# Trace of eight matrix products: Tile's planned order replaced by one section with hand-placed semaphores and a TensorE loop

## The chip, the core and the metric

The kernel runs on one core of one Trainium2 chip. The metric is the device time of one execution in microseconds (us). The engines are TensorE (PE, with its weight loads as PEld), VectorE (DVE), ScalarE (ACT), GpSimd (POOL) and SyncE (SP). Transfers are carried by 16 DMA engines; those that POOL issues convert float32 to bfloat16 on the way.

## The reference

```python
def reference(a, b):                       # a, b: [8, 2176, 2176] float32
    prod = np.matmul(a, b)
    traces = np.diagonal(prod, axis1=1, axis2=2).sum(axis=-1)
    return traces.astype(np.float32)       # [8]
```

The trace of a product needs no product: for each batch it is the sum over i, k of a[i, k] · b[k, i]. So every element of a and b is read once, 303 MB in all, and a has to be transposed against b.

## The kernel before, in words

A matrix of 2176 x 2176 is 17 rows of 128 partitions. For each batch the kernel loads a, transposes it on TensorE into `at` (one buffer, 17 rows of 2176), and multiplies `at` with b, summing.

**Loads.** `fetch` (L70 to L77) issues from POOL, in program order. A batch of a comes as a group of 5 rows (tile `middle`) and a group of 2 x 6 rows (tile `stage`, two buffers, used in turn by a and b); b comes the same way. A transfer of 5 rows is 2720 KB as it lands, one of 12 rows 6528 KB. The order of a batch is a5, a12, b5, b12. A tile is loaded again only when its reader is done: a's when TensorE has transposed it, b's when VectorE has multiplied it. Batch 0 begins with one row by SP (`load_first`, L88, cast on ACT and DVE). The last batch loads a as 12 rows and then 5, and b in groups of 4, 4, 4, 2, 1, 1, 1 rows (`fine`), the last row in three pieces (L273).

**Transposes.** `transpose_group` (L134) transposes 128 x 128 blocks into one of three PSUM tiles: pairs of bf16 words as float32 (L151), the odd rows of a group of b as bf16 (L175). One PSUM tile filled is one copy to `at` in `evacuate` (L117): every fourth on DVE (L121), the others on ACT (L123). A batch with groups of 5 and 6 has 26 copies, 8 for the 5 rows and 18 for the 12.

**Products.** `multiply_reduce` (L126, its work is shown as L128) multiplies and sums rows on DVE, 1.05 us per 1000 elements: the 5 rows, then the 12. It begins when all copies of the batch are done (`copies_end`). In the last batch rows 11, 12 and 13 and part of rows 15 and 16 are multiplied on TensorE instead, as 128 x 128 products summed in `trace_ps` (L287), with some unread matmuls between them (`KEEP_BUSY`). A last DVE product takes the diagonal, a matmul with ones sums over the partitions (L306), DVE adds (L309), SP stores (L312). The sums of the first seven batches pass through a matmul and a DVE addition of their own (L295, L296), which Tile places among the transposes of the last batch.

**Order.** Tile places all waits and the pools' buffers; `issue_after` fixes the order of the loads, of the DVE products after the copies and of the TensorE products. TensorE's program is written out for all eight batches.

Of the kernel before, what the change touches and what calls it, by code (L numbers as in the profile page):

```python
# [8 lines left out]


def row_groups(p, rows):

    groups, at = [], 0
    for m in rows:
        groups.append((at, m))
        at += m * p
    return groups
# [3 lines left out]
def kernel(  # L21
# [6 lines left out]
    nc = tc.nc  # L28
    P = 128
    BATCH, N, N2 = a.shape  # L30
    assert N == N2 and N % P == 0
    NT = N // P
    MOST, MID = 12, 5
# [3 lines left out]
    MUL, ADD = mybir.AluOpType.mult, mybir.AluOpType.add  # L37

    even = [5, 6, 6]
    fine = [4, 4, 4, 2, 1, 1, 1]  # L40

    a_loads = b_loads = [(1, 5), (2, 6)]
    first_loads, last_loads = [(1, 1), (1, 4), (2, 6)], [(2, 6), (1, 5)]
    for loads in (a_loads, first_loads, last_loads):
        assert sum(g * m for g, m in loads) == NT
    assert sum(even) == sum(fine) == NT

    PE_ROWS = (11, 12, 13)

    SHARED_ROW = 15  # L50
    HALF = 8 * P

    LAST_PIECES = [(6 * P, 11 * P, N), (2 * P, 2 * P, 6 * P), (0, 0, 2 * P)]

    KEEP_BUSY = {11: 7, 13: 6, SHARED_ROW: 2}

    const = ctx.enter_context(tc.tile_pool(name="const", bufs=1))
    at_pool = ctx.enter_context(tc.tile_pool(name="at_pool", bufs=1))
    stage = ctx.enter_context(tc.tile_pool(name="stage", bufs=2))
    middle = ctx.enter_context(tc.tile_pool(name="middle", bufs=1))  # L60
    single = ctx.enter_context(tc.tile_pool(name="single", bufs=1))
    psum_pool = ctx.enter_context(tc.tile_pool(name="psum", bufs=3, space=bass.MemoryType.PSUM))
    psum_small = ctx.enter_context(tc.tile_pool(name="psum_small", bufs=1, space=bass.MemoryType.PSUM))

    loaded = []

    def in_order():

        return tc.issue_after(loaded[-1].ins) if loaded else nullcontext()

    def fetch(t, src, start, g, m):

        rows = src[start:start + P * g * m, :].rearrange("(g p r) k -> p g (r k)", g=g, r=m)
        with in_order():
            issued = nc.gpsimd.dma_start(out=t.rearrange("p (g r) k -> p g (r k)", g=g), in_=rows)  # L75
        loaded.append(issued)
        return t  # L77

    def load(src, start, g, m):

        if g * m <= MID:
            t = middle.tile([P, MID, N], bf16, tag="middle")
        else:
            t = stage.tile([P, MOST, N], bf16, tag="stage")
        return fetch(t[:, 0:g * m, :], src, start, g, m)

    def load_first(src, start):

        words = stage.tile([P, MOST, N], bf16, tag="stage")
        plain = words.bitcast(f32).rearrange("p r k -> p (r k)")[:, :N]  # L90
        half = N // 2
        t = single.tile([P, 1, N], bf16, tag="single")
        nc.sync.dma_start(out=plain, in_=src[start:start + P, :])
        nc.scalar.copy(out=t[:, 0, :half], in_=plain[:, :half])  # L94
        nc.vector.tensor_copy(out=t[:, 0, half:], in_=plain[:, half:])  # L95
        return t

    per_batch = len(b_loads)
    tiles = {}

    def constants():
        identity32 = const.tile([P, P], f32, tag="identity32")
        make_identity(nc, identity32)
        identity16 = const.tile([P, P], bf16, tag="identity16")
        make_identity(nc, identity16)
        ones = const.tile([P, 1], f32, tag="ones")
        nc.vector.memset(ones, 1.0)
        sums = const.tile([P, (BATCH - 1) * per_batch], f32, tag="sums")
        late = const.tile([P, 2 * NT], f32, tag="late")
        diagonal = const.tile([P, P], bf16, tag="diagonal")  # L110
        result = const.tile([P, BATCH], f32, tag="result")
        tiles.update(ones=ones, sums=sums, late=late, result=result, diagonal=diagonal)
        tiles[f32], tiles[bf16] = identity32, identity16

    evacs = 0
    last_copy = None

    def evacuate(dst, src):
        nonlocal evacs, last_copy
        if evacs % 4 == 3:  # L120
            last_copy = nc.vector.tensor_copy(out=dst, in_=src)  # L121
        else:
            nc.scalar.copy(out=dst, in_=src)  # L123
        evacs += 1

    def multiply_reduce(x, y, acc, out=None):  # L126

        nc.vector.tensor_tensor_reduce(  # L128
            out=x if out is None else out, in0=x, in1=y, scale=1.0, scalar=0.0,
            op0=MUL, op1=ADD, accum_out=acc,  # L130
        )

    def transpose_group(at, a_t, start, m, b_groups):

        words = a_t.bitcast(f32)
        dst = at[:, :, start:start + P * m].rearrange("q v (p r) -> q v p r", r=m)
        pairs, singles = [], []
        for b_start, bm in b_groups:
            v = b_start // P
            if bm % 2 == 0:  # L140
                for t in range(bm // 2):
                    pairs.append((v + 2 * t, b_start // 2 + t, bm // 2))
            else:
                singles += [(v + r, b_start + r, bm) for r in range(bm)]

        for at0 in range(0, len(pairs), 8 // m):
            some = pairs[at0:at0 + 8 // m]
            ps = psum_pool.tile([P, 8, P], f32, tag="aT")
            for n, (v, c0, step) in enumerate(some):
                for r in range(m):  # L150
                    nc.tensor.transpose(  # L151
                        ps[:, n * m + r, :],
                        words[:, r, c0:c0 + step * (P - 1) + 1:step],
                        tiles[f32],
                    )
            if m == 1:
                v0 = some[0][0]
                evacuate(
                    dst[:, v0:v0 + 2 * len(some), :, 0].rearrange("q (n s) p -> q n s p", s=2),
                    ps.bitcast(bf16).rearrange("q n (p s) -> q n s p", s=2)[:, 0:len(some), :, :],  # L160
                )
                continue
            for n, (v, _, _) in enumerate(some):
                evacuate(
                    dst[:, v:v + 2, :, :],
                    ps[:, n * m:(n + 1) * m, :].bitcast(bf16).rearrange("q r (p s) -> q s p r", s=2),
                )
        for at0 in range(0, len(singles), 16 // m):
            some = singles[at0:at0 + 16 // m]
            ps = psum_pool.tile([P, 8, P], f32, tag="aT")  # L170
            ps16 = ps.bitcast(bf16).rearrange("q a b -> q (a b)")[:, 0:len(some) * m * P]
            ps16 = ps16.rearrange("q (n r p) -> q n r p", r=m, p=P)
            for n, (v, c0, step) in enumerate(some):
                for r in range(m):
                    last_transpose = nc.tensor.transpose(  # L175
                        ps16[:, n, r, :],
                        a_t[:, r, c0:c0 + step * (P - 1) + 1:step],
                        tiles[bf16],
                    )
            v0 = some[0][0]  # L180
            evacuate(dst[:, v0:v0 + len(some), :, :], ps16.rearrange("q n r p -> q n p r"))
        return last_transpose

    pe_work = []

    def multiply_on_pe(at, row, v, lo, hi):

        for c in range(lo, hi, P):
            pe_work.append((at[:, v, c:c + P], row[:, c:c + P]))

    def keep_pe_busy(at, v):

        x = at[:, v, :]
        pe_work.extend([(x[:, 0:P], x[:, 0:4 * P])] * KEEP_BUSY.get(v, 0))

    late = []
    ahead = None
    for bi in range(BATCH):
        last = bi == BATCH - 1
        b_groups = row_groups(P, fine if last else even)  # L200


        at = at_pool.tile([P, NT, N], bf16, tag="at")
        at_row = 0
        for g, m in last_loads if last else a_loads if bi else first_loads:
            start = at_row * P
            at_row += g * m
            if not tiles:
                a_t = load_first(a[bi], start)
                ahead = load(a[bi], start + P * m, *first_loads[1])  # L210
                with tc.issue_after(loaded[-1].ins):
                    constants()
            elif ahead is not None:
                a_t, ahead = ahead, None
            else:
                a_t = load(a[bi], start, g, m)
# [129 lines left out]
```

## Time and profile before

| what | value |
|---|---|
| median of 3 runs | 708.93 us (708.8 to 709.13) |
| span of the profiled execution, first to last instruction | 707.05 us |
| outside the span, median less span | 1.88 us |
| HBM read | 303.04 MB, 429 GB/s over the span |
| PE, PEld, DVE, ACT, POOL busy | 28%, 25%, 55%, 29%, 3% |
| mean granted TensorE clock | 0.656 |
| PE instructions, PEld instructions | 1569, 1569 |

The profile is of one execution. The time of that same execution outside its span is not recorded, so changes are counted in its span and added to the median. A row of the timeline gives start, duration, engine, line, operation, count, and in brackets the idle time before with what ended it. The chain of waits follows the end back, step by step, to what released it. The clock is the share of full speed that TensorE was granted.

### The profile page before, as it was taken

The numbers are of one execution on the slowest core, as the hardware profiler recorded it, in microseconds if no ns is written. First come the engines' busy times: TensorE is split into PE (matmuls) and PEld (weight loads), VectorE is DVE, ScalarE is ACT, GpSimd is POOL, SyncE is SP. The second block draws the span as 40 slices with busy tenths as digits, with TensorE's granted clock in tenths as the row PEclk, the third lists the DMA queues.
The fourth block names the chain that finished last, engine by engine and source line by source line (L and its number), as shares of the span: only waits on it lengthen the run. The fifth ranks groups of instructions, "written<-read, shape, count | busy, mean of one in ns | idle before, by whom it ended". The sixth has DMA issues, their size and how long they took to land.

```text
span 707.1 us, 3653 instructions
## 1 busy us (share of the span) xinstructions
PE 200.8 (28%) x1569; PEld 179.8 (25%) x1569; DVE 386.8 (55%) x98; ACT 202.9 (29%) x160; POOL 24.7 (3%) x47
## 2 busy tenths in 40 slices
PE   2235003450134501344012440134301353003806
PEld 1234002440123401243012430124301343003703
DVE  0105488154881539616397163961629627395497
ACT  2327002470024700346004350044500445002910
POOL 1000000000000000000000000000000000000100
PEclk9759555695557955678556785567755677555957
DMA  9999999999999999999999999999999999999997
GB/s 236 213 217 212 225 206 214 216 224 214 224 215 213 223 213 214 216 223 218 215 217 216 215 222 213 216 223 211 221 216 216 222 214 217 216 220 213 217 211 151
DMA packets 7698, 152.31 MB, mean 215 GB/s; under 512 B 642, under 2 KB 898, under 8 KB 1282
## 3 DMA queue, kind: packets, MB, share of 16 engines
q0 software_dynamic: 7536, 150.96, 99.6%
q1 hardware_dynamic: 146, 1.11, 0.4%
q8 instruction: 12, 0.20, 0.1%
q14 instruction: 4, 0.03, 0.0%
HBM read 303.04 MB, written 0.00 MB: 429 GB/s over the span
## 4 chain that ended last, share of the span: by engine, by line
DVE 33%; another core or an unknown queue 27%; ACT 13%; PE 12%; DMA 11%; issue 3%; POOL 0%; ACTq 0%; DVEq 0%; POOLq 0%
DVE at L128 33%; ACT at L123 13%; PE ps L151 9%; DMA t<-in_a_dram 6%; DMA shared<-in_b_dram 5%; PE ps L175 2%; DVE at L121 0%; POOL shared L75 0%; PE trace_ps L287 0%; POOL shared L273 0%; POOL identity masks.py:199 0%; POOL identity masks.py:197 0%; ACTq L123 0%; DVE diagonal L128 0%
## 5 line engine op out<-in xcount | busy, mean ns | idle before, releaser
L123 ACT COPY at<-ps 128x1536 bf16<-128x1536 bf16 (+5 forms) x158 | 200.5, 1359 | 467.2 <-DVE sums L128 308.6
L128 DVE CUSTOM_DVE_ANT_0 at<-at,t 128x10880 bf16<-128x10880 bf16 (+1 forms) x14 | 272.0, 19426 | 96.3 <-DMA t<-in_b_dram 86.6
L151 PE MATMUL ps<-identity,t 128*128 128x128 f32 x833 | 147.1, 344 | 471.6 <-DMA t<-in_a_dram 378.6
L151 PEld LDWEIGHTS ps<-identity,t 128*128 128x128 f32 x833 | 131.3, 209 | 484.6 <-issue 380.3
L121 DVE COPY at<-ps 128x1536 bf16<-128x1536 bf16 (+3 forms) x52 | 83.4, 1604 | 205.8 <-PE ps L151 152.5
L175 PE MATMUL ps<-identity,t 128*128 128x128 bf16 x646 | 45.8, 227 | 11.0 <-ACT at L123 8.6
L175 PEld LDWEIGHTS <-t 128*128 128x128 bf16 x646 | 43.1, 119 | 14.7 <-issue 14.2
L128 DVE CUSTOM_DVE_ANT_0 at<-at,shared 128x8704 bf16<-128x8704 bf16 (+4 forms) x6 | 29.9, 5001 | 1.8 <-DMA shared<-in_b_dram 1.7
L75 POOL DMA_DIRECT2D t<-in_a_dram x16 | 10.1, 637 | 294.1 <-DVE sums L128 267.4
L75 POOL DMA_DIRECT2D t<-in_b_dram x14 | 8.7, 628 | 290.8 <-PE ps L175 290.5
L287 PEld LDWEIGHTS <-at 128*128 128x128 bf16 x86 | 6.8, 112 | 24.7 <-issue 23.9
L287 PE MATMUL trace_ps<-shared,at 128*128 128x128 bf16 x71 | 5.8, 241 | 21.0 <-DMA shared<-in_b_dram 20.9
L75 POOL DMA_DIRECT2D shared<-in_b_dram x6 | 3.2, 541 | 59.3 <-DVE sums L128 38.9
L287 PE MATMUL unread<-at 128*128 128x512 bf16 x15 | 5.2, 496 | 0.0
L296 DVE TENSOR_REDUCE result<-total 1x7 f32<-1x14 f32 x1 | 0.2, 159 | 7.8 <-PE total L295 7.8
L95 DVE CAST t<-words 128x1088 bf16<-128x1088 f32 x1 | 0.7, 727 | 4.9 <-DMA words<-in_a_dram 4.9
L94 ACT CAST t<-words 128x1088 bf16<-128x1088 f32 x1 | 1.1, 1099 | 3.7 <-DMA words<-in_a_dram 3.7
L273 POOL DMA_DIRECT2D shared<-in_b_dram x3 | 1.6, 552 | 1.9 <-DMA shared<-in_b_dram 1.9
L94 ACT ACT_TABLE_LOAD x1 | 1.3, 1283 | 0.7 <-PEq L330 0.7
L128 DVE DVE_READ_ACCUMULATOR2_ANT sums<- 128x1 f32 x14 | 1.2, 83 | 0.0
L128 DVE CUSTOM_DVE_ANT_0 diagonal<-identity,trace_ps 128x128 bf16<-128x128 f32 x1 | 0.3, 289 | 0.6 <-PE trace_ps L287 0.6
L128 DVE DVE_READ_ACCUMULATOR2_ANT late<- 128x1 f32 x7 | 0.6, 83 | 0.0
(12 smaller groups left out, 2.1 us busy)
## 6 DMA issues: line engine op xcount, KB each, us to landing
t<-in_a_dram POOLq DMA_DIRECT2D x8, 6528.0 KB, 55.1
t<-in_b_dram POOLq DMA_DIRECT2D x7, 6528.0 KB, 52.8
t<-in_b_dram POOLq DMA_DIRECT2D x7, 2720.0 KB, 22.1
t<-in_a_dram POOLq DMA_DIRECT2D x7, 2720.0 KB, 24.8
shared<-in_b_dram POOLq DMA_DIRECT2D x3, 2176.0 KB, 36.0
t<-in_a_dram POOLq DMA_DIRECT2D x1, 2176.0 KB, 14.7
words<-in_a_dram SPq DMA_DIRECT2D x1, 1088.0 KB, 5.0
shared<-in_b_dram POOLq DMA_DIRECT2D x1, 1088.0 KB, 30.5
```

Source lines behind the costliest of these rows:

```text
L75: issued = nc.gpsimd.dma_start(out=t.rearrange("p (g r) k -> p g (r k)", g=g), in_=rows)
L94: nc.scalar.copy(out=t[:, 0, :half], in_=plain[:, :half])
L95: nc.vector.tensor_copy(out=t[:, 0, half:], in_=plain[:, half:])
L121: last_copy = nc.vector.tensor_copy(out=dst, in_=src)
L123: nc.scalar.copy(out=dst, in_=src)
L128: nc.vector.tensor_tensor_reduce(out=x if out is None else out, in0=x, in1=y, scale=1.0, scalar=0.0, op0=MUL, op1=ADD, accum_out=acc,)
L151: nc.tensor.transpose(ps[:, n * m + r, :], words[:, r, c0:c0 + step * (P - 1) + 1:step], tiles[f32],)
L175: last_transpose = nc.tensor.transpose(ps16[:, n, r, :], a_t[:, r, c0:c0 + step * (P - 1) + 1:step], tiles[bf16],)
L273: loaded.append(nc.gpsimd.dma_start(out=row[:, lo:hi], in_=b[bi, start:start + P, lo:hi]))
L287: before = nc.tensor.matmul(trace_ps if real else unread[:, 0:4, :], x, y, start=(n == 0 or not real), stop=(n == len(pe_work) - 1 or not ...
L296: nc.vector.reduce_sum(out=result[:1, 0:done], in_=total[:, 0:early].rearrange("o (b n) -> o b n", n=per_batch), axis=mybir.AxisListType.X,)
```

## The change

The whole kernel stands in one critical section, in which Tile places no waits; every wait and increment is written out on semaphores of its own. All tiles are fixed: `at`, `middle` for the 5 rows, `a_side` and `b_side` for the 12 rows of a and b, three PSUM tiles taken in turn. Groups of b are 5, 6, 6 in all batches. TensorE runs one loop body eight times; it waits on semaphores that count down again, and SP passes each landing of a on to it (`mid_in`, `all_in`). The first row loaded by SP is row 4 of the first 5 rows. In the last batch a is loaded as 5 and then 12 rows, b as 5, 6, 2, 1, 1, 1 rows and the three pieces. There, DVE multiplies rows 0 to 4, 5 to 8, 14, and parts of 15 and 16; TensorE rows 9, 10, 11, 12, 13 and the rest of 15 and 16. The matmul that sums the first seven batches now stands behind the last `at_done`, and DVE's addition of it stands ahead of the last batch's products.

The core of the diff (the new lines; what they replace is the function above):

```python
+    with tc.tile_critical():
+        first = a[0, 0:MID * P, :].rearrange("(p r) k -> p r k", r=MID)
+        nc.sync.dma_start(out=plain, in_=first[:, MID - 1, :]).then_inc(sem["first"], 16)
+        for bi in range(BATCH):
+            nc.sync.wait_ge(sem["a_mid"], 16 * (bi + 1))
+            if bi == 0:
+                nc.sync.wait_ge(sem["cast"], 2)
+            nc.sync.sem_inc(sem["mid_in"], 1)
+            nc.sync.wait_ge(sem["a_all"], 16 * (bi + 1))
+            nc.sync.sem_inc(sem["all_in"], 1)
...
+                nc.gpsimd.wait_ge(sem["product"], 2 * bi - 1)
+                nc.gpsimd.dma_start(
+                    out=middle.rearrange("p (g r) k -> p g (r k)", g=1), in_=group(a[bi], 0, 1, MID),
+                ).then_inc(sem["a_mid"], 16)
+                nc.gpsimd.wait_ge(sem["filled"], per_batch * bi)
+            nc.gpsimd.dma_start(
+                out=a_side.rearrange("p (g r) k -> p g (r k)", g=2),
+                in_=group(a[bi], MID * P, 2, SIDE),
+            ).then_inc(sem["a_all"], 16)
...
+            nc.gpsimd.wait_ge(sem["filled"], per_batch * bi + mid_fills)
+            nc.gpsimd.dma_start(
+                out=middle.rearrange("p (g r) k -> p g (r k)", g=1), in_=group(b[bi], 0, 1, MID),
+            ).then_inc(sem["b_mid"], 16)
...
+        def evacuate(engine, copy, bi, dve):
+            mine = [i for i in range(per_batch) if on_dve(bi, i) == dve]
+            for i in mine:
+                moves, dst, src = fills[i]
+                engine.wait_ge(sem["filled"], bi * per_batch + i + 1)
+                if bi and i == mine[0]:
+                    engine.wait_ge(sem["product"], 2 * bi)
+                copy(out=dst, in_=src).then_inc(sem[f"free{i % BUFS}"], 1)
+            engine.drain().then_inc(sem["at_done"], 1)
...
+        for bi in range(BATCH):
+            evacuate(nc.vector, nc.vector.tensor_copy, bi, True)
+            nc.vector.wait_ge(sem["at_done"], 2 * (bi + 1))
+            nc.vector.wait_ge(sem["b_mid"], 16 * (bi + 1))
+            if bi == BATCH - 1:
+                break
...
+        nc.vector.wait_ge(sem["summed"], 1)
+        nc.vector.reduce_sum(
+            out=result[:1, 0:BATCH - 1],
+            in_=total[:, 0:2 * (BATCH - 1)].rearrange("o (b n) -> o b n", n=2),
+            axis=mybir.AxisListType.X,
+        )
...
+        rows_product(0, middle, column())
+        nc.vector.wait_ge(sem["b_all"], 16 * BATCH)
+        rows_product(MID, b_side[:, 0:DVE_ROWS, :], column())
+        slot = SIDE - LAST
+        nc.vector.wait_ge(sem["piece2"], 16)
+        rows_product(DVE_ROW, b_side[:, DVE_ROW + slot:DVE_ROW + slot + 1, :], column())
+        nc.vector.wait_ge(sem["piece3"], 16)
+        multiply_reduce(at[:, SHARED_ROW, HALF:], b_side[:, SHARED_ROW + slot, HALF:], column())
...
+        with nc.Fori(0, BATCH, engines=(PE,)):
+            for i, (moves, _, _) in enumerate(fills):
+                if i == 0:
+                    nc.tensor.wait_ge(sem["mid_in"], 1).then_inc(sem["mid_in"], -1)
+                if i == mid_fills:
+                    nc.tensor.wait_ge(sem["all_in"], 1).then_inc(sem["all_in"], -1)
+                free = sem[f"free{i % BUFS}"]
+                nc.tensor.wait_ge(free, 1).then_inc(free, -1)
+                for into, block, identity in moves:
+                    done = nc.tensor.transpose(into, block, identity)
+                done.then_inc(sem["filled"], 1)
+
+        nc.tensor.wait_ge(sem["at_done"], 2 * BATCH)
+        nc.tensor.wait_ge(sem["product"], early)
+        nc.tensor.matmul(total[:, 0:early], ones, sums, start=True, stop=True).then_inc(
+            sem["summed"], 1
+        )
...
+    with tc.tile_critical():
+        nc.sync.wait_ge(sem["out"], 16)
```

## The prediction

> **What bounds the kernel now.** I read the page's slices and queues first.
>
> ```profile
> DMA  9999999999999999999999999999999999999997
> GB/s 236 213 217 212 225 206 214 216 224 214 224 215 213 223 213 214 216 223 218 215 217 216 215 222 213 216 223 211 221 216 216 222 214 217 216 220 213 217 211 151
> ...
> q0 software_dynamic: 7536, 150.96, 99.6%
> ...
> q8 instruction: 12, 0.20, 0.1%
> ```
>
> The DMA engines are busy in every slice but the last. Bytes set the time, so an edit counts only if it moves the first transfer, adds or removes traffic, lets the queue run dry, or lengthens what follows the last bytes. The chain of waits shows whether the queue runs dry in a steady batch:
>
> ```profile
> 212.42 10.01 another core or an unknown queue
> 222.42 0.14 issue
> 222.56 6.83 PE ps L151 x36
> ...
> 242.76 11.49 DVE at L128
> 254.26 11.78 another core or an unknown queue
> ```
>
> At 212.4 TensorE is done with the 5 rows of a and POOL issues all of b; a's 12 rows are still landing for another 10.0 us. So loads are issued 10 us early, and neither kernel waits for an issue in the middle. The second reading: from the first transpose of the 12 rows to the start of the DVE product, the 18 copies take 242.76 - 222.56 = 20.2 us.
>
> Then the tail, in the timeline:
>
> ```profile
> 651.50 0.16 DVE L296 TENSOR_REDUCE result<-total 1x7 f32<-1x14 f32 x1 [7.82 <-PE total L295]
> ...
> 672.03 9.21 DVE L128 CUSTOM_DVE_ANT_0 at<-at,shared 128x8704 bf16<-128x8704 bf16 x1
> ...
> 690.97 6.96 DVE L128 CUSTOM_DVE_ANT_0 at<-at,shared 128x6528 bf16<-128x6528 bf16 x1 [0.57 <-DMA shared<-in_b_dram]
> ...
> 698.71 2.43 DVE L128 CUSTOM_DVE_ANT_0 at<-at,shared 128x2176 bf16<-128x2176 bf16 x1 [0.77 <-DMA shared<-in_b_dram]
> ...
> 701.21 1.36 DVE L128 CUSTOM_DVE_ANT_0 at<-at,shared 128x1152 bf16<-128x1152 bf16 x1
> ...
> 702.93 0.83 DVE L128 CUSTOM_DVE_ANT_0 at<-at,shared 128x640 bf16<-128x640 bf16 x1 [0.35 <-DMA shared<-in_b_dram]
> ...
> 704.34 0.29 DVE L128 CUSTOM_DVE_ANT_0 diagonal<-identity,trace_ps 128x128 bf16<-128x128 f32 x1 [0.58 <-PE trace_ps L287]
> ```
>
> DVE starts at 672.0 and from 691 on waits for landings (0.57, 0.77, 0.35 us), so it keeps pace with the loads. The last transfer lands at 703.54 by the chain; the diagonal product follows at 704.34 and the span ends at 707.05.
>
> **What the change leaves alone.** The bytes are the same, and the packets nearly so. By the trace's packet records a 26112 B packet takes 1942 ns, 21760 B 1622, 17408 B 1302, 4352 B 342. The last b becomes 128 packets of each of the first, second and last kind, in place of 384 of the third: 128 x (1942 + 1622 + 342 - 3 x 1302) ns = 0. The copies, their 3-to-1 split between ACT and DVE, the three PSUM tiles and the release points of `middle` and the 12-row buffers are those of before. POOL's waits guard the same readers, so the 10 us of cover stay; even 5 us more on an issue would be hidden. POOL now issues its second load ahead of the identities, at nothing: the first load is still moving (14.7 us to landing).
>
> **What moves: the last batch.** Before, a's 12 rows came first and its 5 rows last, so only 8 copies and a small group stood behind the last landing of a. Now a is in the steady order, and the 12 rows land last. When? One batch after the previous 12 rows: their first transpose was at 572.78, the period is 309.86 - 222.56 = 87.30, so 660.1. Batch 7 gives DVE seven copies, as the 222.56 batch had, so I take its 20.2: copies done at 680.3. Behind that DVE must do 5 rows (11.49), 4 rows (9.14, the step from the first 8704-element row to the next, 672.03 to 681.17), row 14 (2.50, from 698.71 to 701.21), 1152 elements (1.36) and 640 (0.83): 25.3 us. 680.3 + 25.3 = 705.6 for the diagonal product, which stood at 704.34: **+1.26 us**, because DVE, not the last landing, is now late. TensorE isn't: 6 rows still follow when b's group of 6 has landed, at 2.57 us each (a 12-row load is 16 packets of 1.94 us per engine less their overlap, 30.8 us), so it lands near 688; then 34 products cost 3.9 us cold (17 took 1.97), seven fillers 3.2, and the remaining rows follow their landings as before.
>
> **New hand-offs, all ahead of that DVE chain.** For each, value and both ends:
> - Start: a second barrier of sequencers before SP's first load, at 0.74. The row for one such step is the gap from the release at 0.66 to that load, 0.08 us; the whole first barrier took 0.66. Value 0.15, ends 0 and 0.6. POOL's first load hides behind SP's row, which moves until 5 us.
> - SP passes on a's landing: two semaphore steps. Semaphore steps in the chain are 0.02 to 0.14. Value 0.15, ends 0.05 and 0.5.
> - TensorE's own count-down wait for each of 18 copies, where the wait used to ride on the matmul. An event instruction on TensorE lasts 0.05; copies on ACT hide most. Value 0.2, ends 0 and 1.8 (18 x 0.1).
> - The copies' end now passes a drain on ACT and DVE, then a TensorE matmul, then DVE's addition for the first seven batches, before any product. At the end of the kernel the same pair runs from the accumulator read at 704.56 to the end of the addition at 705.08, 0.44 us after that read's 0.08; with the drain 0.65. Before, it stood at 651.50, beside copies, and cost nothing. Ends 0.3 and 1.2.
> - End: a second section and its barrier around the store. Most passes while the store flies (0.32 us issue at 705.11, landing 1.1 us later). Value 0.2, ends 0 and 0.6.
>
> **The loop's fetches.** The page counts 12 instruction packets on q8 of 16 KB; with 3138 PE and PEld instructions that is one per 262. Each packet took about 0.95 us of one DMA engine, 11.3 us in all, spread over 16: 0.7 us. They also set the engines apart: in the packet records a transfer's first and last engine ended within 0.43 us at the start of the run and within 2.3 us near its end. A body of 187 transposes is 374 instructions plus some 28 waits, 1.5 packets. If it stays resident the fetches go, and a's last landing comes up to 1.9 us (two packets on the slowest engine) sooner. If the body is fetched at each turn, 16 to 24 packets replace 12: 0.24 to 0.7 us more on the mean, up to 1.5 on the slowest engine. Value +0.3, ends -1.9 and +1.5. I take the refetch: the old program fetched steadily, at one packet per 262 executed instructions from 57.6 us on, so a turn's first half is probably gone at its end. The turn's branch itself falls into TensorE's idle time (the 12 rows are transposed by 591, the next use is past 640), so its delay costs nothing there.
>
> [...]
>
> **Sum.** 1.26 + 0.15 + 0.15 + 0.2 + 0.65 + 0.2 + 0.3 = 2.9 us. The span becomes 709.95; with the 1.88 us that lie between this span and the median, **711.8 us**, 0.4% slower. All lows give 1.26 + 0.05 + 0.3 - 1.9 = -0.3 (708.6), all highs 1.26 + 0.6 + 0.5 + 1.8 + 1.2 + 0.6 + 1.5 = 7.5 (716.4).
>
> **Rivals.**
> - *The body stays resident (0.15).* Fetch term -1.9 in place of +0.3: 709.6. For: 400 instructions are little beside 3100. Against: the steady fetching. On the other side of my forecast: not slower than the measurement can tell, and deciding from a gain of about 1.5 us at a's last landing.
> - *DVE is not late (0.08).* If copies, hand-offs or products run about 2.5 us shorter together, the last landing decides again and only start, end and fetch remain: 708.93 + 0.65 = 709.6. Against: product durations repeat to 0.01 us (11.49 in every batch).
> - *The loop stalls inside a turn (0.12).* If the second half of the body is fetched only when TensorE gets there, in the transposes of the 12 rows, the wait (a 1.94 us data packet ahead, 0.95 for the fetch, about 1 for issue and landing) adds near 4 us to the last copies: 715.7. In earlier batches the 10 us of cover hide it.
> - *Faster (0.05).* The fetches go and every hand-off sits at its low end: 708.6 by the sum; a gain over 0.2% would need 1.1 us more from the copies, whose 18 took 19.7 us in other batches (329.56 - 309.86), half of it.
>
> **Chances.** The forecast has the remaining 0.60, with 710.4 to 713.5 its own range. 0.2% (1.4 us), about what a measurement of this kernel can tell from no change, puts the line at 710.35. Slower: 0.60 + 0.12 + 0.02 of the first two rivals = 0.74. Same: 0.21, the rest of those. Faster: 0.05. For 8 in 10, I go from 709.0, leaving out only the faster case and a little of the resident one, to 714.8, leaving out most of the stall.
>
> **What would show it.** Right: in the last batch the DVE products follow one another without waiting for landings, from about 681.7 to a diagonal product near 707.0, while the trace products on PE end before; the addition of seven results stands directly before the first of them; the first transpose of the last 12 rows is near 660.7. q8 has 16 to 24 packets. Wrong: if DVE waits for `b_side` pieces at the end, the DVE term falls; if q8 has 2 to 4 packets, the fetch term; if the first landing moves by over 0.6 us, or a slice in the middle loses its 9 for the DMA, I have overlooked a wait in the steady batches.

## The result, and the profile after

| | before | after |
|---|---|---|
| median | 708.87 us (708.8 to 709.13) | 712.86 us (712.52 to 713.01) |
| span of the profiled execution | 707.05 | 710.91 |
| instruction packets on q8 | 12 | 2 |
| end of the last load's packets, by the packet records | 703.55 | 702.65 |
| diagonal product on DVE | 704.34 | 704.86 |
| store issued by SP | 705.11 | 705.62 |
| from there to the end of the span | 1.94 | 5.30 |

The ratio is 1.0055, with a 95% interval of 1.0042 to 1.0067: 4.0 us slower, over the 0.2% that a measurement of this kernel can tell. The forecast of 711.8 us has the right sign and nearly the size, but most of its size for the wrong reason, as the table shows: most of the loss is in the last row, behind the store.

The page of the changed kernel, slices and queues:

```profile
DMA  9999999999999999999999999999999999999995
GB/s 232 215 215 220 215 207 229 215 206 226 211 215 225 211 224 214 213 224 214 220 219 213 221 216 215 220 216 208 229 212 212 226 207 222 217 211 221 217 207 100
...
q0 software_dynamic: 7536, 150.96, 99.1%
...
q8 instruction: 2, 0.03, 0.0%
```

The DMA engines are busy in every slice but the last, as before, and no slice shows the queue dry. Only the last slice is emptier, so the added time lies behind the last landing. The 12 instruction packets on q8 are down to 2.

The timeline of its last batch (start, duration, engine, line, operation; idle time and its cause in brackets):

```profile
659.24 6.63 PE L305 MATMUL fill<-identity,a_side 128*128 128x128 f32 x36 [9.17 <-PEq L303]
...
679.85 0.16 DVE L259 TENSOR_REDUCE result<-total 1x7 f32<-1x14 f32 x1 [1.47 <-PE total L310]
679.94 11.48 DVE L229 CUSTOM_DVE_ANT_0 at<-at,middle 128x10880 bf16<-128x10880 bf16 x1
...
691.35 9.22 DVE L229 CUSTOM_DVE_ANT_0 at<-at,b_side 128x8704 bf16<-128x8704 bf16 x1
...
700.49 2.42 DVE L229 CUSTOM_DVE_ANT_0 at<-at,b_side 128x2176 bf16<-128x2176 bf16 x1
...
702.84 1.35 DVE L229 CUSTOM_DVE_ANT_0 at<-at,b_side 128x1152 bf16<-128x1152 bf16 x1
...
704.86 0.28 DVE L229 CUSTOM_DVE_ANT_0 diagonal<-identity,trace_ps 128x128 bf16<-128x128 f32 x1
...
705.62 0.32 SPq L147 DMA_DIRECT2D out_dram<-result  x1
```

The DVE products follow one another with no wait in brackets: the chain of DVE is the end, no longer the landings. The addition of the seven results stands directly ahead of them. But all of it is some 2 us earlier than forecast, and the store is only 0.51 us later than before. The rest is in SP's waits (engine, line, what it waited for; total, times, longest). Before, SP's waits at the kernel's end (L341) were short, and one of them was for the store itself:

```profile
SPq L341 <- PEq L341: 0.6, 2, 0.5
SPq L341 <- DMA out_dram<-result: 0.4, 1, 0.4
```

After:

```profile
SPq L147 <- DVE result L287: 46.7, 1, 46.7
SPq L135 <- POOLq L135: 3.0, 1, 3.0
```

L135 is the section. At its end SP collects all engines and waits 3.0 us for POOL. What POOL does there is a drain. The drains behind the last copies ended just after the work before them on their engines: ACT's ran from 677.09 to 679.46 us and ended 0.03 us after its last copy, DVE's from 677.44 to 678.43 and ended 0.05 us after its own. Drains count as idle and stand in no row of the timeline; the trace's records have them (start and duration in ns):

```
before   670489  35034  GpSimd DRAIN   (kernel's end, L341)
after    706016   3250  GpSimd DRAIN   (section's end, L135)
```

In both kernels POOL drains after its last load. Before, nothing held that drain back: it began at 670.5, lasted until 705.52, 2.0 us past the last packet of the loads, and SP's store was not over before 706.2. In the changed kernel it starts only when SP signals that it has reached the section's end, at 705.98. By then all loads have landed for some 3 us, and it still takes 3.25 us.

### The profile page after: what moved, and what is told of

Same layout as the page of the kernel before. It is cut to its first block, busy times and chain, and to the rows that moved or that the text cites. A ratio compares the mean times of both kernels' runs of the same rounds, so it can differ in the third digit from the quotient of the medians.

```text
span 710.9 us, 3916 instructions
## 1 busy us (share of the span) xinstructions
PE 205.3 (29%) x1624; PEld 186.2 (26%) x1626; DVE 382.2 (54%) x96; ACT 202.4 (28%) x158; POOL 25.0 (4%) x47
## 3 DMA queue, kind: packets, MB, share of 16 engines
q0 software_dynamic: 7536, 150.96, 99.1%
## 5 line engine op out<-in xcount | busy, mean ns | idle before, releaser
L216 ACT COPY at<-fill 128x1536 bf16<-128x1536 bf16 (+3 forms) x156 | 200.0, 1371 | 472.2 <-DVE sums L229 356.7
L229 DVE CUSTOM_DVE_ANT_0 at<-at,b_side 128x26112 bf16<-128x26112 bf16 (+4 forms) x11 | 205.1, 18665 | 83.5 <-DMA b_side<-in_b_dram 83.5
L216 DVE COPY at<-fill 128x1536 bf16<-128x1536 bf16 (+2 forms) x52 | 83.9, 1614 | 221.0 <-PE fill L305 220.6
L305 PE MATMUL fill<-identity,middle 128*128 128x128 f32 (+1 forms) x440 | 68.3, 339 | 371.2 <-PEq L303 371.2
L305 PEld LDWEIGHTS fill<-identity,middle 128*128 128x128 f32 (+1 forms) x440 | 63.2, 180 | 376.1 <-issue 375.7
L305 PE MATMUL fill<-identity,a_side 128*128 128x128 f32 (+1 forms) x1056 | 123.6, 276 | 114.3 <-PEq L303 113.7
L305 PEld LDWEIGHTS fill<-identity,a_side 128*128 128x128 f32 (+1 forms) x1056 | 113.5, 167 | 124.4 <-issue 124.0
L229 DVE CUSTOM_DVE_ANT_0 at<-at,middle 128x10880 bf16<-128x10880 bf16 x8 | 91.9, 11490 | 11.0 <-ACTq L217 11.0
L342 PE MATMUL trace_ps<-b_side,at 128*128 128x128 bf16 x105 | 8.7, 249 | 10.5 <-DMA b_side<-in_b_dram 10.4
L187 POOL DMA_DIRECT2D b_side<-in_b_dram x7 | 5.0, 712 | 0.0
L198 POOL DMA_DIRECT2D b_side<-in_b_dram x4 | 2.1, 563 | 0.0
L203 POOL DMA_DIRECT2D b_side<-in_b_dram x3 | 1.6, 593 | 0.0
```

What stands on the lines that cost most here:

```text
L187: nc.gpsimd.dma_start(out=b_side.rearrange("p (g r) k -> p g (r k)", g=2), in_=group(b[bi], MID * P, 2, SIDE),).then_inc(sem["b_all"], 16)
L198: nc.gpsimd.dma_start(out=b_side[:, SIDE + r:SIDE + r + m, :].rearrange("p r k -> p (r k)"), in_=rows[:, r:r + m, :].rearrange("p r k -> p ...
L203: nc.gpsimd.dma_start(out=b_side[:, MOST - 1, lo:hi], in_=rows[:, SIDE - 1, lo:hi],).then_inc(sem[f"piece{len(LATE_SLICES) + k}"], 16)
L216: copy(out=dst, in_=src).then_inc(sem[f"free{i % BUFS}"], 1)
L229: return nc.vector.tensor_tensor_reduce(out=x if out is None else out, in0=x, in1=y, scale=1.0, scalar=0.0, op0=MUL, op1=ADD, accum_out=acc,)
L305: done = nc.tensor.transpose(into, block, identity)
```

## Experiments

Kernels are built on the changed kernel unless said otherwise. The kernel before had a median of 708.99 us beside them. The changed kernel was not measured again with them: its 712.86 us stood beside 708.87 us of the kernel before, so a difference from it can be off by that 0.1 us.

### POOL's drain ahead of the section's end

```diff
                 ).then_inc(sem[f"piece{len(LATE_SLICES) + k}"], 16)
+        nc.gpsimd.drain()
```

> The changed kernel, with a drain of POOL directly behind its last load. Theory A: the 3.25 us drain of POOL at the end of the section is work left over from its loads; the old kernel had it beside the last landings (its drain began at 670.5 and ended at 705.5), and it can lie there again. Then the new drain runs from 655 to about 705, the section's own drain of POOL is under 0.2 us, and the time falls by about 3 us, to 709.7. Theory B: 3.25 us is what leaving such a section costs on POOL, whatever was drained ahead. Then the time stays at 712.9 and the long drain stays at 706.

710.05 us, 1.0013 (1.0004 to 1.0023) of the kernel before, 2.8 us less than the changed kernel. The early drain lasted from 652.50 to 704.63, the section's own took 0.04 us. Of SP's waits these two remain at the end; the line of L135 with POOL is gone:

```profile
SPq L147 <- DVE result L288: 46.6, 1, 46.6
SPq L380 <- PEq L380: 0.7, 2, 0.6
```

Theory A holds, and with it 2.8 of the 4.0 us are found.

### The kernel before, with its drain held back

```diff
+    copied = const.tile([1, BATCH], f32, tag="copied")
+    nc.gpsimd.tensor_copy(out=copied, in_=tiles["result"][:1, :BATCH])
     nc.sync.dma_start(
         out=out.rearrange("(a b) -> a b", a=1),
```

> The old kernel, with a copy of the eight results on POOL behind the last addition, so that POOL's drain at the end of the kernel can begin only after it. Theory A: the drain loses its cover and takes about 3 us after the copy, from 705.5 to 708.7, where the store was over at 706.2: some 2.6 us more, 711.5. Theory B (the price belongs to the section): only the copy is added, 0.3 us at most, 708.9 to 709.2.

711.29 us, 1.0031 (1.0019 to 1.0043). POOL's drain went from 670.5 to 705.51 and took 3.48 us there, with the wait for the 0.18 us copy in it. From the store (705.49) to the end of the span (709.74) it is now 4.25 us, where it was 1.94. So the price does not belong to the section: one small instruction of POOL behind the loads was enough to expose it.

### What the drain's length depends on

```diff
+            if last:
+                nc.gpsimd.drain()
             nc.gpsimd.wait_ge(sem["filled"], per_batch * bi + mid_fills)
```

> The changed kernel with a drain of POOL ahead of the last batch's loads of b, so that 9 of 39 loads are left for the drain at the section's end. It holds POOL until a has landed, so the load queue runs dry and the total time rises by several us; only the length of the last drain is read here. If the drain's 3.25 us is work per load, the last one takes near 3.25 x 9 / 39 = 0.8 us; if it is a fixed price after any loads, 3.25 us again.

One run of 714.24 us. The last drain took 0.79 us with 9 loads since the drain before it, against 3.25 with 39: 82 ns for each load (2.46 us over 30 loads), and 0.05 us besides. A third point agrees: the section's drain of `early_drain`, with no load since the drain before it, took 0.04. So in these runs its length grew with the number of loads. Their packets don't fit as well: the 9 loads are 1296 of 7536 packets, which would leave a fixed 0.28 us for a drain with none. SP's wait at the section's end shrank with the drain, from 3.0 us to 0.5:

```profile
SPq L135 <- POOLq L135: 0.5, 1, 0.5
```

The drain in the middle lasted from 603.9 to 660.2, 1.6 us past the last packet of a (658.64), and the loads of b were issued only then. The queue ran dry, with a DMA share of 0.39 and 0.54 in two stretches (in each row length, busy time and count by engine, then TensorE clock, DMA share, GB/s):

```profile
655.00:660.00 5.00, 0.75 (x4) 0.78 (x5) 0.00 (x0) 0.00 (x0) 0.00 (x0) 0.50 0.39 84
660.00:664.00 4.00, 4.00 (x22) 4.00 (x21) 1.76 (x1) 2.07 (x2) 3.30 (x7) 0.56 0.54 87
```

### TensorE's loop written out

```diff
-        with nc.Fori(0, BATCH, engines=(PE,)):
+        for _ in range(BATCH):
```

> The changed kernel, with TensorE's eight batches written out instead of looped, the same waits. Theory: the loop body stayed resident, which took the instruction packets on q8 from 12 to 2 and let the last 12 rows of a land about 0.9 us sooner. Then written out there are 12 or more such packets again, the first transpose of the last 12 rows moves from 659.2 to about 660.1, and as DVE's products are the end, the time rises by as much, to 713.8. Rival: the landing came sooner for another reason (order of the loads); then 712.9 with 12 packets.

714.09 us, 1.007 (1.0057 to 1.0084): 1.2 us more than with the loop. Its page and its timeline:

```profile
q8 instruction: 13, 0.21, 0.1%
```

```profile
660.42 6.70 PE L305 MATMUL fill<-identity,a_side 128*128 128x128 f32 x36 [9.17 <-PEq L303]
...
681.12 11.48 DVE L229 CUSTOM_DVE_ANT_0 at<-at,middle 128x10880 bf16<-128x10880 bf16 x1
...
706.05 0.28 DVE L229 CUSTOM_DVE_ANT_0 diagonal<-identity,trace_ps 128x128 bf16<-128x128 f32 x1
```

The packets are back, the last 12 rows of a come 1.18 us later and the diagonal product 1.19 us. By the packet records, the slowest DMA engine ended the load of those rows 2.58 us after the fastest in this kernel, 1.39 us with the loop: the same 1.19 us. So the loop gains, by what it takes off the slowest engine, and the rival falls. The body stays resident, that is, it is not fetched again at a turn: with the loop q8's two packets start at 57.7 us, in the first pass of the body, and at 691.0, behind the last, and none between.

### One row less for DVE

```diff
-    DVE_ROWS = 4
+    DVE_ROWS = 3
```

> The changed kernel, with one row of the last b (row 8) moved from DVE to TensorE. Theory: DVE's chain from the last copies sets the diagonal product at 704.86, 0.6 us or so past what the last landing (702.6) and TensorE would allow. Then one row less, 2.27 us of DVE, brings the diagonal product to about 703.9 (the last trace products end near 703.3), and the time falls by about 1 us, to 711.9; the drain of POOL still follows. Rival: landing or TensorE sets the end already; then 712.9, or more if the 17 added products make TensorE late.

711.32 us, 1.0034 (1.0021 to 1.0048): 1.5 us less than the changed kernel. The chain of waits is again one of landing and TensorE:

```profile
653.66 48.88 DMA b_side<-in_b_dram
702.55 0.05 issue
702.60 0.69 PE trace_ps L342 x6
703.29 0.02 issue
703.31 0.29 DVE diagonal L229
```

DVE's chain was the bound ahead of the store, by 704.86 - 703.31 = 1.55 us, half a microsecond more than expected: TensorE's last products end near 703.3 as expected, but the diagonal product follows them within 0.02 us.

### The hand-off ahead of the products

```diff
-        nc.vector.wait_ge(sem["summed"], 1)
-        nc.vector.reduce_sum(
-            out=result[:1, 0:BATCH - 1],
...
                 multiply_reduce(at[:, NT - 1, lo:mid], b_side[:, MOST - 1, lo:mid], column())
+        nc.vector.wait_ge(sem["summed"], 1)
+        nc.vector.reduce_sum(
+            out=result[:1, 0:BATCH - 1],
...
         nc.vector.wait_ge(sem["traced"], 1)
```

> The changed kernel, with DVE's addition of the first seven batches moved behind the last batch's products (TensorE's matmul for it stays where it is). Theory: the hand-off from the last copy over TensorE to DVE's addition, 0.5 us from the end of ACT's last copy to the first product, stands on the path; without it the first product starts about 0.4 us sooner, the addition's 0.2 us come back at the end, and the time falls by 0.2 to 0.3 us, to 712.6. Rival: the drain of ACT alone holds the product; then nothing moves.

712.51 us, 1.0048 (1.0032 to 1.0063); the interval is too wide to tell 0.3 us from the changed kernel. The timeline can:

```profile
679.63 11.49 DVE L229 CUSTOM_DVE_ANT_0 at<-at,middle 128x10880 bf16<-128x10880 bf16 x1 [1.11 <-ACTq L217]
```

By the records ACT's last copy ended at 679.56 here and at 679.43 in the changed kernel. From there to the first product it is 0.07 us in place of 0.51: the hand-off over TensorE and the addition costs 0.44 us on the path, and the drain next to nothing. The store is issued at 705.39 in place of 705.62, the 0.2 us that were expected.

### Both repairs together, looped and written out

`early_dve3` has the early drain and three rows for DVE; `early_dve3_unrolled` also has TensorE written out.

> The changed kernel with both edits that helped: POOL's drain directly behind its last load, and row 8 of the last b on TensorE. Theory: two separate prices on one path, the late drain (2.8 us when taken away alone) and DVE's chain (1.5 us alone), so they add: 712.86 - 2.8 - 1.5 = 708.5, just under the kernel before. Rival: with the chain shorter by 1.5 us, the early drain (which ends some 2 to 3 us after the last landing at 702.6) is itself the end; then the section's drain of POOL still shows a rest of 0.5 to 1.5 us past 704.5, and the time is 709 to 710.

> The kernel of early_dve3 with TensorE's eight batches written out. Theory: the loop's gain is the instruction packets that the DMA engines no longer carry (2 in place of 12 or 13), so it holds where the last landing is the end as well: the last landing moves from 702.6 to about 703.9 and the time rises by 1.0 to 1.3 us, to 709.7. Rival: the gain is seen only where a's landing decides, and the end pieces, which land within 1.3 us of each other anyway, even it out; then under 0.3 us is lost.

`early_dve3`: 708.64 us, 0.9994 (0.9985 to 1.0003) of the kernel before: level with it, not shown to be faster. The two prices add (712.86 - 2.8 - 1.5). The rival has no part in the time: the early drain ended at 704.47, 0.15 us after SP's signal of 704.32, but SP comes to ask for POOL only at 704.72, and from the store to the end of the span it is 2.40 us, as in `early_drain`.

`early_dve3_unrolled`: 709.79 us, 1.0011 (1.0002 to 1.002), 1.15 us more, measured side by side. The landing in which the chain ends, with the loop and written out:

```profile
653.76 48.68 DMA b_side<-in_b_dram
702.44 0.05 issue
```

```profile
654.25 49.66 DMA b_side<-in_b_dram
703.91 0.05 issue
```

So the packets' price is nearly the same where the landing decides (1.15 us, 1.23 where DVE's chain did); the rival that the small last pieces even it out falls.

## Why the prediction was right and wrong, step by step

**What bounds, and what is left alone: right.** The DMA slices stay at 9 up to the last, TensorE still waits 9 to 10.5 us for a's 12 rows in every batch behind the first (9.17 in the last), so the loads are issued as early as before, and the packets on q0 are the same 7536.

**The order of a and DVE's chain: right in kind.** Forecast were 20.2 us for the 18 copies, 0.65 for the hand-off, 25.3 for the products. Measured: 20.2 (659.24 to ACT's end at 679.43), 0.51, and 24.92 (679.94 to 704.86). The hand-off's 0.65 was 0.44 for the pair and 0.21 for the drain; `sums_late` gives 0.44 and 0.07. The products came 0.4 us shorter, since each starts beside the 0.08 us accumulator read of the one before it, which the forecast counted in for most of them. `dve3` shows that this chain was the bound.

**Start and SP's hand-on: right.** The first packet moved from 1.76 to 1.98, 0.22 us for a forecast of 0.15. From the last packet of a's 12 rows to the first transpose it is 0.62 us (658.62 to 659.24) where it was 0.49 in the kernel before (646.75 to 647.24): 0.13 for 0.15.

**TensorE's count-down waits: nothing seen** in place of 0.2. The 18 copies take 20.2 us as before; the waits were not tried by themselves.

**The loop's fetches: wrong.** The step reads "I take the refetch", +0.3. From one packet per 262 executed instructions I concluded that old instructions are given up as new ones come. The runs show 2 packets and the body resident, as the forecast's own sign for this had it ("if q8 has 2 to 4 packets, the fetch term"); against the written-out kernel that gains 1.2 us. That row came from a program that ran straight on and could not tell the two apart, and I should have given residence more than 0.15. No fetch on q8 stands at a turn: the branches of TensorE's seven turns stand between 65.84 and 589.86 us and took 0.22 us each. How long a body can be and still stay resident, no run shows.

**The end: wrong, and the largest error.** "End: a second section and its barrier around the store ... Value 0.2, ends 0 and 0.6." It measured 3.36 us (5.30 less 1.94). The step looked at SP's barriers and not at what each engine does on leaving. The row was in the trace of before: a POOL drain of 35 us, from the last load to 2 us past the last landing. Drains count as idle there, so the step did not ask what had hidden it. `early_drain` gives 2.8 us of the 3.36; the remaining half microsecond `early_drain` keeps (2.40 us from store to end, against 1.94). By its records 0.37 us of that lie between the store's landing (706.80) and the kernel's own exit (707.20), in the steps by which SP leaves the second section, and 0.11 in a longer clearing of the semaphores (222 ns against 114). A kernel without the second section was not tried.

**The sum.** Ahead of the diagonal product +0.52 in place of +2.7, behind it +3.34 in place of +0.2. The two errors, -1.5 us on the fetches (with 0.7 in smaller terms) and +3.1 at the end, partly cancelled, so it is luck that the number is off by 1.1 us only. With the end's error alone it would have been 711.8 + 3.1 = 714.9, at the upper end of the range; the written-out kernel, which lacks the loop's gain, measured 714.09. That upper end was set by a stall in the loop, of which no run shows anything.

## What to carry to other kernels

Before putting work in a section with a joint exit, list what each engine drains on leaving it, and what hid that before; give an engine that issued many loads its drain right behind its last one (2.8 us here, for 39 loads). A loop whose body stays resident can take instruction packets off the DMA engines: this one of some 400 instructions left 2 on q8 in place of 13, and as these engines were the bound, the last landing of a came 1.18 us earlier, by what the slowest engine no longer carried. Of a chain that ends late, try to move a piece to an engine that waits for landings: here one row brought back 1.5 us.

## What the runs showed of the hardware

- A drain of GpSimd that began after its loads had landed took about 82 ns for each load since the last drain (3.25 us for 39 in the changed kernel, 0.79 for 9 in `mid_drain`, 0.04 for none in `early_drain`). Three that began while loads were moving lasted until 1.6 to 2.0 us behind their last packet (from 603.9 to 660.20 against 658.64 in `mid_drain`, from 652.5 to 704.63 against 702.68 in `early_drain`, from 670.5 to 705.52 against 703.55 in the kernel before).
- An instruction packet of 16 KB took 0.89 to 1.0 us of one DMA engine, and the engine stayed behind: with 12 packets the engines' ends drifted from 0.4 to 2.3 us apart over a run, with the changed kernel's one packet ahead of the tail (57.7 us) they stayed at 1.4 from there to the last small pieces.
- A TensorE loop of 374 instructions and some 28 waits, run eight times, fetched nothing on q8 at its turns (2 packets, at 57.7 and 691.0 us; 13 with the same work written out).
